# The gate's partition sums of a conditioned short-convolution layer: one fp32 product with ones, or two fp32r products of a high and a low part

## The chip, the core and the metric

The kernel runs on one core of a Trainium2 chip. The core has a matmul engine (PE, whose weight loads are listed apart as PEld), a vector engine (DVE), an activation engine (ACT), GpSimd (POOL), and a queue that issues DMAs (SP). The metric is the device time of one execution in microseconds (us); the median of the runs of a kernel is compared. TensorE is another name for PE.

## What is computed

The reference, cut to the parts that this case runs (one layer, batch 1, 256 rows of 2048):

```python
h = rmsnorm(x, norm_g[0])
mod = silu(c) @ ada_w[0] + ada_b[0]            # 2048 -> 3 * 2048
shift, scale, gate = split(mod, 3)
h = h * (1.0 + scale) + shift
b, cg, v, g = split(h @ sc_w_in[0], 4)         # 2048 -> 4 * 4096
y = b * causal_conv(cg * v, conv_w) * silu(g)  # width 3
x = x + gate * (y @ sc_w_out[0])               # 4096 -> 2048
return rmsnorm(x, final_g)
```

All arrays are float32. The change touches only `gate`: the last third of `silu(c) @ ada_w`, a vector of 2048, which the kernel needs in every partition, since the 256 rows lie in partitions when the gate is applied.

## The kernel before, in words

**Large products.** Each float32 operand is split into a high part, written as fp32r by an ACT cast (`split_hi`, line 318), and a low part, the difference written as fp32r by DVE (`split_lo`, line 323). A product of two operands is then three matmuls: high by high, high by low, low by high (`product`, line 429, and `out_mm`, lines 613 to 615). Weights arrive 1 MB at a time in tiles `raw`, `hi` and `lo` that have three buffers each.

**Stages.** First x is normalized, transposed and modulated with the first shift and scale values. Then comes the first half of the input projection (bank tile `mm_s`), in an order that `plan` works out and that interleaves the shift and scale pieces of `ada_w` (`ada_piece`, line 390 and following). Then comes its second half, a loop over 16 tiles of channels in pairs and the four quarters (`mm_b`, lines 557 to 591), 32 turns in all. The output projection follows in four column blocks dc of 512 (`mm_o`, lines 635 to 690), each over eight pieces of `w_out`.

**The gate.** Each turn of the second half calls `gate_piece` once (line 576). There are 32 pieces: for each of the four column blocks dc, eight pieces of two 128-row blocks of `ada_w`. A piece takes a tile `at_g` from the pool `adap` (tag `at`, four buffers of 1024 floats per partition, shared with the shift and scale pieces, which come before), loads 512 KB into it (line 540, on SP), and adds silu(c) times each of its two rows to the partial sums `gacc` (lines 547 and 549, DVE). `gacc` has tag `gv`, two buffers. After the eighth piece of a block, one matmul of a 128x128 tile of ones with `gacc` adds the 128 partitions up and leaves the sum in every partition (line 552, bank tile `ps_gate`, two buffers shared with other small tiles). DVE adds the bias to it (line 553), and the result, `gate(dc)`, is read at lines 676 (blocks 0 to 2) and 657 (block 3).

**Order.** The instructions of each engine stand in the order that a scheduler gives them when the program is built: it keeps a simulated time, and takes among the instructions that are ready the one with the earliest place in the program. `gate_sums` is called inside `later(GIVE)`, which places its instructions 300 places later than they are written, so that they fill time that is left. On the chip each engine then follows that order.

Of the kernel before, what the change touches and what calls it, by code (L numbers as in the profile page):

```python
# [8 lines left out]
F32 = mybir.dt.float32  # L9
F32R = mybir.dt.float32r  # L10
AF = mybir.ActivationFunctionType
ALU = mybir.AluOpType

P = 128
# [103 lines left out]
def short_conv_layer(ctx: ExitStack, tc: tile.TileContext, x, c, norm_g, ada_w, ada_b, w_in, conv_w, w_out, final_g, out):  # L118
    nc = tc.nc
# [6 lines left out]
    const = ctx.enter_context(tc.tile_pool(name="const", bufs=1))  # L126
    const.tile([P, 48], F32, tag="line0", name="line0")
    adap = ctx.enter_context(tc.tile_pool(name="adap", bufs=2))
# [77 lines left out]
    for n, (j, kk) in enumerate(((0, 4), (4, 4), (8, 4), (12, 2), (14, 1), (15, 1))):  # L206
        at = wpool.tile([P, SLOT], F32, tag=("lo", "hi")[n % 2], name="at0", bufs=3)[:, : kk * 2 * NK0 * P]
        at = at.rearrange("p (k s f) -> p k s f", k=kk, s=2)
# [10 lines left out]

    ident = const.tile([P, P], F32, tag="ident", name="ident")  # L220
    make_identity(nc, ident)
    ones = const.tile([P, P], F32, tag="ones", name="ones")
    nc.vector.memset(ones, 1.0)
    eps_t = const.tile([P, 1], F32, tag="eps", name="eps_t")
    nc.vector.memset(eps_t, EPS)

# [33 lines left out]
    for t in range(TT):  # L260
        for dh in range(2):
# [3 lines left out]
            else:  # L265
                nc.vector.scalar_tensor_tensor(
                    out=junk[:, t], in0=xt[t][dh], scalar=1.0, in1=xt[t][dh], op0=ALU.mult, op1=ALU.mult,
# [58 lines left out]
    def split(raw, n, lo_tag="lo"):  # L326

        return split_lo(raw, n, split_hi(raw, n), lo_tag)
# [4 lines left out]
    gv0 = adap.tile([P, 2, 2 * P], F32, tag="gv", name="gv0")[:, :, 0 : NK0 * P]  # L333
    turn_x(0, 4)

    def sum0(k, rows, col, halves=(0, 1)):


        for o in range(2 * NK0):
            if o // NK0 in halves:  # L340
                nc.tensor.matmul(
                    sums0[:, o * P : (o + 1) * P], rows[:, o // NK0, (o % NK0) * P : (o % NK0 + 1) * P],
                    col.to_broadcast([P, P]),
                    start=k == min(IDLE_AT) and o == 0, stop=k is None, skip_group_check=True,
                )

    for k in range(KT):
        c_k = silu_c[:, k : k + 1]
        at, gv = first_ada[k], gv0
        if k in IDLE_AT:  # L350
# [4 lines left out]
            at, gv = at[:, 1], gv0[:, 1]  # L355
# [2 lines left out]
        else:  # L358
            nc.vector.scalar_tensor_tensor(out=gv, in0=at, scalar=c_k, in1=gv, op0=ALU.mult, op1=ALU.add)
    for half in range(2):  # L360
        sum0(None, gv0, ones[:, 0:1], (half,))
    pieces0 = [split(raw0[:, 0 : CT * P], CT * P)]
    hi0 = [split_hi(raw0[:, k * CT * P : (k + 1) * CT * P], CT * P) for k in range(1, NK0)]
    modulate(0, NK0, sums0.rearrange("p (o f) -> p o f", o=2 * NK0)[:, :, 0])
# [159 lines left out]
    def gate(dc):  # L524
        return gates[dc // 2][:, dc % 2, :]
# [4 lines left out]
    def gate_piece():  # L530
        if not gate_todo:
            return
        dc, j = gate_todo.pop(0)
        at = adap.tile([P, ASLOT], F32, tag="at", name="at_g", bufs=4)
        at3 = at.rearrange("p (k f) -> p k f", k=2)
        with later(GIVE):
            gate_sums(dc, j, at3)

    def gate_sums(dc, j, at3):
        nc.sync.dma_start(at3, adas[:, j : j + 2, 2, dc * 512 : (dc + 1) * 512])  # L540
        if j == 0:
            gacc[0] = adap.tile([P, 512], F32, tag="gv", name="gacc")
        ga = gacc[0]
        for i in range(2):
            s = silu_c[:, j + i : j + i + 1]
            if j + i == 0:
                nc.vector.tensor_scalar_mul(ga, at3[:, i, :], s)
            else:
                nc.vector.scalar_tensor_tensor(out=ga, in0=at3[:, i, :], scalar=s, in1=ga, op0=ALU.mult, op1=ALU.add)
        if j + 2 == KT:  # L550
            ps = psum.tile([P, 512], F32, tag="sm", name="ps_gate", bufs=2)
            nc.tensor.matmul(ps, ones, ga, start=True, stop=True)  # L552
            nc.vector.tensor_tensor(out=gate(dc), in0=ps, in1=gate(dc), op=ALU.add)

    KP = 8
# [79 lines left out]
    for dc in range(4):  # L635
# [10 lines left out]
        for ep in range(n_ep):  # L646
# [7 lines left out]
            if dc == 3:  # L654
# [3 lines left out]
                    out=raw3, in0=raw3, in1=gate(dc).unsqueeze(1).to_broadcast([P, EP, 512]), op=ALU.mult  # L658
# [57 lines left out]
```

## Time and profile before

| | us |
|---|---|
| median of three runs | 925.61 |
| lowest, highest run | 924.23, 926.99 |
| the profiled execution | 925.65 |
| its span, first to last instruction | 923.9 |
| PE busy (98% of the span) | 905.0 |
| DVE busy (67%) | 614.7 |
| ACT busy (50%) | 466.2 |
| the four gate products (line 552), busy as listed | 3.9 |
| gate sums on DVE (lines 547 and 549), 64 instructions | 46.9 |

A group of instructions is one line of the program on one engine with one shape; "x8" is how many there were. A matmul's listed duration runs to a modelled end and overlaps with the next matmul, so what a matmul costs in a stream is read from the distance between starts, or from the chain, the sequence of work traced back from the last instruction. One fp32 matmul in the program shows as two passes in the trace: the four gate products are eight.

### The profile page before, as it was taken

What the parts mean: (1) busy time and instruction counts of PE and PEld (TensorE: products, weight loads), DVE (VectorE), ACT (ScalarE), POOL (GpSimd) and SP (SyncE); (2) the same over time, 40 slices, a digit from 0 to 9 for tenths busy, and PEclk for the clock granted to TensorE, in tenths of its full rate; (3) what the DMA queues carried; (4) which work ended last, traced back from release to release, by engine and by line L of the source; (5) the groups of instructions that cost most, each with busy time, mean ns of one, the idle gap of its engine ahead of it and who ended that gap; (6) DMA issues with size and microseconds to landing.
All of it is one profiled execution on the core that took longest, in us unless ns stands there. A gap on an engine that the chain in (4) does not pass through costs nothing.

```text
span 923.9 us, 16438 instructions
## 1 busy us (share of the span) xinstructions
PE 905.0 (98%) x7135; PEld 870.0 (94%) x7135; DVE 614.7 (67%) x593; ACT 466.2 (50%) x417; POOL 0.7 (0%) x6
## 2 busy tenths in 40 slices
PE   7999999999999999999999999999999999999996
PEld 7898999999999999999999999999999988888885
DVE  4798989897686899875554554455454544545882
ACT  3785876655557856644334333443344333443333
POOL 0000000000000000000000000000000000000000
PEclk9999999999999999999999999999999999999999
DMA  9999999999985789676656665666556496566542
GB/s 314 339 362 326 339 367 366 341 373 357 314 294 180 236 297 355 228 241 205 191 185 197 202 192 185 195 204 194 184 185 199 141 343 225 185 208 200 183 136 92
DMA packets 163753, 227.66 MB, mean 246 GB/s; under 512 B 5680, under 2 KB 104160, under 8 KB 163296
## 3 DMA queue, kind: packets, MB, share of 16 engines
q1 hardware_dynamic: 163440, 226.51, 74.1%
q8 instruction: 56, 0.92, 0.4%
q14 instruction: 17, 0.14, 0.0%
q10 hardware_dynamic: 240, 0.09, 0.0%
HBM read 224.49 MB, written 2.10 MB: 245 GB/s over the span
## 4 chain that ended last, share of the span: by engine, by line
PE 90%; DMA 5%; DVE 2%; issue 1%; SPq 1%; ACT 0%; ACTq 0%; DVEq 0%
PE mm_b L429 38%; PE mm_s L429 33%; PE mm_o L615 6%; PE mm_o L614 6%; PE mm_o L613 6%; DMA at<-in_ada_w_dram 3%; DMA raw_s<-in_sc_w_in_dram 1%; DVE lo L323 1%; DVE gv L412 1%; DMA x<-in_x_dram 1%; PE ps_gate L552 0%; SPq L215 0%; PE tp_g L419 0%; ACT hi L318 0%; DVE gv L410 0%
## 5 line engine op out<-in xcount | busy, mean ns | idle before, releaser
L429 PE MATMUL mm_s<-hT,hi 128*128 128x256 f32 x2048 | 351.7, 277 | 1.6 <-ACT hT L310 1.1
L429 PE MATMUL mm_b<-hT,hi 128*128 128x256 f32 x2048 | 348.8, 276 | 0.0
L429 PEld LDWEIGHTS mm_s<-hT,hi 128*128 128x128 f32 x2048 | 309.6, 189 | 2.5 <-ACT hT L310 1.3
L429 PEld LDWEIGHTS mm_b<-hT,hi 128*128 128x128 f32 x2048 | 308.4, 188 | 0.2 <-issue 0.2
L429 PE MATMUL mm_s<-hT,lo 128*128 128x256 f32 x1024 | 283.6, 278 | 4.0 <-DVE lo L323 3.9
L429 PE MATMUL mm_b<-hT,lo 128*128 128x256 f32 x1024 | 282.6, 276 | 0.0
L323 DVE TENSOR_TENSOR lo<-raw,hi 128x2048 fp32r<-128x2048 f32 (+1 forms) x66 | 148.1, 2244 | 134.6 <-ACT hi L318 134.6
L318 ACT CAST hi<-raw 128x2048 fp32r<-128x2048 f32 (+1 forms) x66 | 123.7, 1874 | 209.0 <-PE mm_b L429 153.3
L429 PEld LDWEIGHTS mm_s<-hT,lo 128*128 128x128 f32 x1024 | 192.5, 188 | 5.2 <-DVE lo L323 4.8
L429 PEld LDWEIGHTS mm_b<-hT,lo 128*128 128x128 f32 x1024 | 192.2, 188 | 0.2 <-issue 0.2
L323 DVE TENSOR_TENSOR lo<-raw_s,hi 128x2048 fp32r<-128x2048 f32 (+1 forms) x80 | 147.9, 1850 | 36.0 <-ACT hi L318 35.2
L318 ACT CAST hi<-raw_s 128x2048 fp32r<-128x2048 f32 (+1 forms) x80 | 124.5, 1557 | 72.3 <-PE mm_s L429 49.1
L323 DVE TENSOR_TENSOR lo<-raw_o,hi 128x2048 fp32r<-128x2048 f32 x32 | 73.3, 2291 | 64.9 <-ACT hi L318 64.9
L318 ACT CAST hi<-raw_o 128x2048 fp32r<-128x2048 f32 x32 | 61.0, 1907 | 106.9 <-PE mm_o L615 83.4
L614 PE MATMUL mm_o<-lo,y 128*128 128x512 f32 x256 | 99.7, 391 | 0.0
L613 PE MATMUL mm_o<-hi,y 128*128 128x512 f32 x256 | 99.3, 389 | 0.0
L615 PE MATMUL mm_o<-hi,y 128*128 128x512 f32 x256 | 99.3, 389 | 0.0
L412 DVE SCALAR_TENSOR_TENSOR gv<-at,silu_c,gv 128x512 f32<-128x512 f32 x105 | 78.5, 750 | 5.5 <-DMA at<-in_ada_w_dram 3.9
L450 ACT COPY acc<-mm_s 128x1024 f32<-128x1024 f32 x54 | 54.6, 1012 | 36.8 <-PE mm_s L429 36.8
L614 PEld LDWEIGHTS mm_o<-lo,y 128*128 128x128 f32 x256 | 48.1, 188 | 10.2 <-issue 0.2
L615 PEld LDWEIGHTS mm_o<-hi,y 128*128 128x128 f32 x256 | 48.0, 188 | 10.0 <-issue 0.2
L613 PEld LDWEIGHTS mm_o<-hi,y 128*128 128x128 f32 x256 | 48.0, 188 | 10.0
(90 smaller groups left out, 368.1 us busy)
## 6 DMA issues: line engine op xcount, KB each, us to landing
raw<-in_sc_w_in_dram SPq DMA_DIRECT2D x64, 1024.0 KB, 5.6
raw_s<-in_sc_w_in_dram SPq DMA_DIRECT2D x47, 1024.0 KB, 8.1
raw_o<-in_sc_w_out_dram SPq DMA_DIRECT2D x32, 1024.0 KB, 5.3
at<-in_ada_w_dram SPq DMA_DIRECT2D x114, 256.0 KB, 7.6
raw_s<-in_sc_w_in_dram SPq DMA_DIRECT2D x33, 512.0 KB, 5.8
at_g<-in_ada_w_dram SPq DMA_DIRECT2D x32, 512.0 KB, 7.9
at<-in_ada_w_dram SPq DMA_DIRECT2D x6, 512.0 KB, 8.8
x<-in_x_dram SPq DMA_DIRECT2D x4, 512.0 KB, 6.0
```

The source lines that it names most:

```text
L318: nc.scalar.copy(hi[:, :n], raw[:, :n])
L323: nc.vector.tensor_tensor(out=lo[:, :n], in0=raw[:, :n], in1=hi[:, :n].bitcast(F32), op=ALU.subtract)
L412: nc.vector.scalar_tensor_tensor(out=gv, in0=at4[:, i], scalar=c_k, in1=gv, op0=ALU.mult, op1=ALU.add)
L429: mm = last_mm[0] = nc.tensor.matmul(dst, w, h[:, k], start=begins and left, stop=ends, skip_group_check=True)
L450: nc.scalar.copy(acc[ch, q], bank)
L613: nc.tensor.matmul(po, yh, hi[:, o], start=opens, stop=False, skip_group_check=True)
L614: nc.tensor.matmul(po, yh, lo[:, o], start=False, stop=False, skip_group_check=True)
L615: nc.tensor.matmul(po, yl, hi[:, o], start=False, stop=ct == NCT - 1, skip_group_check=True)
```

## The change

The tile of ones becomes fp32r. At the end of a block's sums ACT copies `gacc` into the first half of a new tile `parts` as fp32r (the high part), DVE writes the difference into its second half (the low part), and two fp32r products with ones, one of each part, are accumulated in `ps_gate`. The tile `parts` has tag `at`, so it takes one of the four buffers that the pieces of `ada_w` are loaded into. Elsewhere `ones` is read as float32, as before.

```diff
-    ones = const.tile([P, P], F32, tag="ones", name="ones")
-    nc.vector.memset(ones, 1.0)
+    ones = const.tile([P, P], F32R, tag="ones", name="ones")
+    nc.vector.memset(ones.bitcast(F32), 1.0)
...
-        sum0(None, gv0, ones[:, 0:1], (half,))
+        sum0(None, gv0, ones[:, 0:1].bitcast(F32), (half,))
...
             ps = psum.tile([P, 512], F32, tag="sm", name="ps_gate", bufs=2)
-            nc.tensor.matmul(ps, ones, ga, start=True, stop=True)
+            parts = adap.tile([P, 2, 512], F32R, tag="at", name="gate_hl", bufs=4)
+            nc.scalar.copy(parts[:, 0], ga)
+            nc.vector.tensor_tensor(out=parts[:, 1], in0=ga, in1=parts[:, 0].bitcast(F32), op=ALU.subtract)
+            for i in range(2):
+                nc.tensor.matmul(ps, ones, parts[:, i], start=i == 0, stop=i == 1)
             nc.vector.tensor_tensor(out=gate(dc), in0=ps, in1=gate(dc), op=ALU.add)
```

## The prediction

> **What bounds the kernel now.** I read the profile's page first: the busy shares, the granted clock by slices, and the shares of the chain that ended last.
>
> ```profile
> PE 905.0 (98%) x7135; PEld 870.0 (94%) x7135; DVE 614.7 (67%) x593; ACT 466.2 (50%) x417; POOL 0.7 (0%) x6
> ...
> PEclk9999999999999999999999999999999999999999
> ...
> PE 90%; DMA 5%; DVE 2%; issue 1%; SPq 1%; ACT 0%; ACTq 0%; DVEq 0%
> ```
>
> PE is busy for 98% of the span at full granted clock, and 90% of the chain is PE. That is an average, so I read the chain in order of time around the four gate products (columns: start, length, work, matmul passes).
>
> ```profile
> 251.76 62.61 PE mm_s L429 x552
> 314.38 1.72 PE ps_gate L552 x4
> 316.09 76.20 PE mm_s L429 x672
> 392.29 292.17 PE mm_b L429 x2578
> 684.46 0.86 PE ps_gate L552 x2
> 685.32 56.02 PE mm_b L429 x494
> ...
> 763.34 0.86 PE ps_gate L552 x2
> ```
>
> From 251.76 to the last gate product the chain never leaves PE. The four products stand in it in full: two together at 314.38, one at 684.46, one at 763.34. What the change frees on PE there, it frees at the end, unless PE begins to wait. Next, therefore, the waits: those of PE alone between 105 and 740 us, then two of the whole run (total, times, longest).
>
> ```profile
> PE mm_s L429 <- DVE lo L323: 1.2, 1, 1.2
> ...
> DVE lo L323 <- ACT hi L318: 234.8, 112, 7.1
> ACT hi L318 <- PE mm_b L429: 159.8, 48, 4.4
> ```
>
> PE waits once, 1.2 us in 635. The dependence runs the other way: ACT waits 159.8 us for PE to free a high-part buffer, and DVE waits for ACT. The makers of operands stand a full ring of buffers ahead, and that ring is the cover for whatever DVE and ACT get in addition.
>
> **The change part by part.** *Removed:* four fp32 products. Their chain time is 1.72 + 0.86 + 0.86 = 3.44 us, or 0.43 us for each of eight passes.
>
> *Added on PE:* eight fp32r products over 512 columns. The trace has this form in the output projection, where operands are fp32r and each product is one pass of 128x512 (256 of each line). I take the spacing from starts in the timeline:
>
> ```profile
> 759.77 0.39 PE L614 MATMUL mm_o<-lo,y 128*128 128x512 f32 x1
> ...
> 762.49 0.39 PE L614 MATMUL mm_o<-lo,y 128*128 128x512 f32 x1
> 762.72 0.39 PE L615 MATMUL mm_o<-hi,y 128*128 128x512 f32 x1
> 762.95 0.39 PE L613 MATMUL mm_o<-hi,y 128*128 128x512 f32 x1
> 763.17 1.02 PE L552 MATMUL ps_gate<-gacc,ones 128*128 128x512 f32 x2
> 763.63 0.79 PE L614 MATMUL mm_o<-lo,y 128*128 128x512 f32 x1
> ```
>
> The two L614 rows are twelve passes apart (the three lines in turn, four times): 2.72 / 12 = 0.227 us. The listed 0.39 overlaps with the next pass and is no price. Eight passes then take 1.82 us, and PE is relieved by 3.44 - 1.82 = **1.62 us**. The bounds: at the dear end the new pass costs what an old one did, 0.43 us, and nothing is gained; at the cheap end it costs what the 256-column passes of the input projection do, 76.20 / 672 = 0.113 us by the chain, and 8 x 0.113 = 0.91 makes the gain 2.53 us. I take 0.227, since it is the same shape and type.
>
> The Trainium skill (TensorE: Matmul & The Clock Gate, "Back-to-back issue gap") gives a sustained spacing of some 131 ns for 512 columns in a stream of weight loads and matmuls; by that the eight would take an estimated 1.05 us and the gain would be 2.39 us. The trace's 0.227 us in just such a stream disagrees, and the measurement decides.
>
> *Added on ACT and DVE:* four casts and four subtracts of 128x512. Their forms are in the trace as the split of y; the third row is one addition of the gate sums.
>
> ```profile
> L382 ACT CAST y<-z 128x512 fp32r<-128x512 f32 x8 | 4.9, 610 | 0.0
> L383 DVE TENSOR_TENSOR y<-z,y 128x512 fp32r<-128x512 f32 x8 | 5.5, 686 | 0.0
> L549 DVE SCALAR_TENSOR_TENSOR gacc<-at_g,silu_c,gacc 128x512 f32<-128x512 f32 x60 | 45.0, 750 | 1.8 <-DMA at_g<-in_ada_w_dram 1.0
> ```
>
> That is 4 x 0.61 = 2.4 us on ACT and 4 x 0.69 = 2.7 us on DVE. I cost them at nothing: ACT is idle half the span. DVE is tighter in one stretch, so I asked for busy times there (columns: stretch, length, PE, PEld, DVE, ACT, POOL, then clock, DMA share, GB/s).
>
> ```profile
> 277.00:300.00 23.00, 23.00 (x205) 23.00 (x205) 14.27 (x17) 17.03 (x19) 0.00 (x0) 1.00 0.60 182
> ...
> 340.00:392.00 52.00, 52.00 (x461) 52.00 (x460) 48.52 (x54) 34.97 (x34) 0.00 (x0) 1.00 0.89 305
> 392.00:741.00 349.00, 349.00 (x3076) 348.52 (x3075) 186.42 (x141) 142.40 (x107) 0.00 (x0) 1.00 0.61 193
> ```
>
> Even at 93% DVE, between 340 and 392, PE does not wait. If that cover were gone, all of the copy and subtract, 4 x (0.61 + 0.69) = 5.2 us, would be the price.
>
> *New waits.* The subtract waits for the copy at the head of DVE's queue, and the next `lo` and gate additions are queued behind it; the copy can itself stand behind an ACT cast that waits for PE, up to 4.4 us by the wait rows. While ACT waits so, PE still has a ring of finished operands to work through; the wait ends by PE's progress, so it costs nothing. The product waits for the low part, and behind it on PE stand all large matmuls; that is priced among the rivals.
>
> *Moved:* `parts` takes one of the four `at` buffers from the end of a block's sums until its second product is done. The rows of SP's queue and of DVE show what this ring does now:
>
> ```profile
> 271.85 1.94 SPq L540 DMA_DIRECT2D at_g<-in_ada_w_dram  x2
> 277.76 42.06 SPq L472 DMA_DIRECT2D raw_s<-in_sc_w_in_dram  x12
> 321.32 0.37 SPq L540 DMA_DIRECT2D at_g<-in_ada_w_dram  x1
> ...
> 270.29 3.11 DVE L549 SCALAR_TENSOR_TENSOR gacc<-at_g,silu_c,gacc 128x512 f32<-128x512 f32 x4
> ...
> 317.81 0.48 DVE L547 TENSOR_SCALAR gacc<-at_g,silu_c 128x512 f32<-128x512 f32 x1
> ```
>
> The sums of block 1 end at 273.40; block 2 begins only at 317.81, after the products at 314.38 have freed a `gacc`, and loads pause meanwhile. Afterwards the split frees `gacc`, so block 2 may begin before 314; but one or two of the four buffers are then held by `parts` until a product runs, so the gate loads go on with fewer buffers and may spread past 392, where DMA runs at 193 GB/s and DVE is at 53%. Either way they move between stretches in which PE does not wait. On SP a gate load that waits for a buffer holds up the weight loads behind it; their cover is the same ring of three. I cost the move at nothing and keep its failure as a rival.
>
> *The sum.* The profiled execution took 925.65 us (span 923.9 and 1.75 around it), which is the median of 925.61 within 0.04. 925.65 - 1.62 = **924.0 us**, 0.18% less. About 0.3%, or 2.8 us, is what a measurement of this kernel can tell from no change; its three runs lie 2.8 us apart.
>
> **The rivals.**
>
> *A. Nothing saved, 925.6.* PE gains 1.62 us and gives it back in a small wait elsewhere, or the new passes cost 0.43. For it: the order of all engines from 240 us on is made anew. Against it: a single PE wait in 635 us.
>
> *B. Cheaper passes, about 923.1.* The bound of 0.113 us. Against it stand the twelve passes of the same shape at 0.227.
>
> *C. The low part comes late: slower.* PE keeps its order, so if a product is placed soon after its sums, PE stands until cast and subtract are done: worst, behind a full cast and a full low part,
>
> ```profile
> L318 ACT CAST hi<-raw 128x2048 fp32r<-128x2048 f32 x64 | 122.4, 1913 | 201.0 <-PE mm_b L429 153.3 <-issue 43.5 <-PE mm_s L429 4.2
> L323 DVE TENSOR_TENSOR lo<-raw,hi 128x2048 fp32r<-128x2048 f32 x64 | 146.7, 2292 | 134.6 <-ACT hi L318 134.6
> ```
>
> 1.91 + 0.61 + 2.29 + 0.69 = 5.5 us. Once gives 924.0 + 5.5 = 929.5, twice 935. It decides when a product stands less than 5.5 us behind the end of its sums, and makes the kernel slower by over 0.3% from 4.4 us of such waits on. Against it: the products before stood far behind (block 1's sums end at 273.40, its product is in the group at 314.38). For it: blocks 2 and 3 may now be summed late.
> The Trainium skill (TensorE: Matmul & The Clock Gate, the table of specifications) calls ACT's and DVE's queues strictly first in, first out, with only weight loads pulled ahead on PE; by that rule this stall could not be worked around.
>
> *D. Gate loads fall into the opening of the output projection: slower.* There DMA is full and a cast already waits for `w_out`:
>
> ```profile
> 745.00:760.00 15.00, 15.00 (x67) 12.39 (x67) 6.39 (x4) 4.86 (x3) 0.00 (x0) 1.00 1.02 400
> ...
> 756.24 1.91 ACT L318 CAST hi<-raw_o 128x2048 fp32r<-128x2048 f32 x1 [7.46 <-DMA raw_o<-in_sc_w_out_dram]
> ...
> 758.18 2.29 DVE L323 TENSOR_TENSOR lo<-raw_o,hi 128x2048 fp32r<-128x2048 f32 x1 [7.08 <-ACT hi L318]
> ```
>
> That low part is done at 760.47 and first used at 763.63 (the L614 row above): 3.2 us of cover. Eight gate pieces of 512 KB there are 4.2 MB, 10.5 us at 400 GB/s, of which 7.3 reach PE: 931.3; five pieces give 927.4. Against it: block 3 can go on loading once block 2's product is done, near 684.
>
> **How the numbers follow.** Forecast 0.72, A 0.12, B 0.04, C 0.07, D 0.05. The likeliest gives 924.0. The bounds of the pass put the time between 923.1 and 925.65. Before's runs scatter by 1.4 us to either side, a median by less: I reach 0.5 below the lower bound, and 1.35 above the upper, which takes in scatter and a stall short of C's: 922.6 to 927.0. Left out are C, most of D and some scatter. Faster by over 0.3% (under 922.8) needs B and luck, or scatter: 0.05. Slower by over 0.3% (over 928.4) is most of C and D: 0.10. Within 0.3%: 0.85.
>
> **What would show it.** In the profile after: line 552's successors are eight passes, 0.227 us apart where they follow each other, 1.8 us in the chain in place of 3.44; the four casts and subtracts near 0.61 and 0.69 us; PE's waits after 105 us still near 1.2 us in all; gate loads spread differently, and none around 745 to 760. A: passes 0.43 us apart, or a new row "PE ... <- DVE". C: PE waiting for the low part of the gate sums. D: gate loads after 735 and PE waiting for a low part of `w_out`. I am wrong if the chain leaves PE between 252 and 900 us for more than 2 us, or if the stretch before 200 us, which the change does not reach, turns out otherwise.

## The result, and the profile after

The kernel after has a median of **932.29 us** (930.08 to 936.42, six runs) against 925.29 us before (923.42 to 926.99, six runs): a ratio of 1.0079 [1.0053, 1.0104], 7.0 us slower. The profiled execution took 930.08 us, the lowest of its six. From the page of after: busy shares, shares of the chain.

```profile
PE 904.6 (97%) x7135; PEld 870.5 (94%) x7135; DVE 616.8 (66%) x597; ACT 468.5 (50%) x421; POOL 0.7 (0%) x6
PE 87%; DMA 6%; DVE 3%; issue 1%; ACT 1%; SPq 1%; ACTq 0%; DVEq 0%
```

PE is busy for as long as before (904.6 against 905.0 us) in a span of 928.3 us against 923.9, and 3% of the chain has moved from PE to DMA, DVE and ACT. So PE stands somewhere. The chain of after in order of time shows where; before, PE alone filled it from 251.76 to 392.29.

```profile
249.80 0.44 PE tp_g L419 x4
250.24 43.48 PE mm_s L429 x383
...
293.77 0.16 DVE gacc L549
...
294.83 1.22 DVE lo L323
...
301.57 4.81 DMA at_g<-in_ada_w_dram
...
310.96 1.15 DVE lo L323
...
312.12 6.02 DMA raw_s<-in_sc_w_in_dram
...
318.22 1.90 ACT hi L318
320.12 0.93 ACT mm_s L462
...
321.09 76.44 PE mm_s L429 x672
...
397.53 292.40 PE mm_b L429 x2580
689.93 0.23 PE ps_gate L556
...
768.18 0.46 PE ps_gate L556 x2
```

Two things are to be seen. The gate products are cheaper: 0.23 us a pass at 690 (where a second one follows) and at 768. And between 293.72 (250.24 + 43.48) and 321.09 the chain leaves PE, for gate sums, gate loads (`at_g`), a late low part, a late weight load and a late cast. At 321.09 PE still has 672 passes to go to the second half (`mm_b`), as it had before at 316.09, and `mm_b` begins at 397.53 in place of 392.29. The waits of PE and of its weight loads (PEld) between 250 and 330 us (us in all, times, longest; before has none of these rows, and between 330 and 392 neither kernel has one):

```profile
PEld mm_s L429 <- DVE lo L323: 4.5, 3, 2.3
PE mm_s L429 <- DVE lo L323: 3.9, 3, 2.1
...
PEld mm_s L429 <- ACT mm_s L462: 2.8, 1, 2.8
...
PE mm_s L429 <- ACT mm_s L462: 2.5, 1, 2.5
```

DVE's rows there show what a low part stands behind (start, length, work; in brackets the idle time before it and what ended it):

```profile
279.32 0.49 DVE L547 TENSOR_SCALAR gacc<-at_g,silu_c 128x512 f32<-128x512 f32 x1 [2.01 <-DMA at_g<-in_ada_w_dram]
...
292.31 0.75 DVE L549 SCALAR_TENSOR_TENSOR gacc<-at_g,silu_c,gacc 128x512 f32<-128x512 f32 x1 [3.02 <-DMA at_g<-in_ada_w_dram]
...
294.83 1.22 DVE L323 TENSOR_TENSOR lo<-raw_s,hi 128x1024 fp32r<-128x1024 f32 x1
```

Block 2's sums begin at 279.32, not at 317.81: the split has read `gacc`, so its buffer is free early. And they wait for their loads: 3.02 us at 292.31, and the low part of 294.83 stands behind that addition. SP's queue tells why the loads are late:

```profile
271.51 1.40 SPq L540 DMA_DIRECT2D at_g<-in_ada_w_dram  x2
...
280.63 0.37 SPq L540 DMA_DIRECT2D at_g<-in_ada_w_dram  x1
...
283.29 2.99 SPq L540 DMA_DIRECT2D at_g<-in_ada_w_dram  x2
```

A piece's load goes out when an earlier piece has been added: at 280.63, behind the two additions of the first piece; at 283.29, when those of the second end (282.52 + 0.74 in the timeline). The load of 283.29 is the one for which DVE waits until 292.31. Only two of the four `at` buffers turn over. The other two hold the `parts` of blocks 0 and 1, written from 241.7 on, until their products, which stand where they stood:

```profile
L556 PE MATMUL ps_gate<-gate_hl,ones x8: 387/397/398, 314.8 to 768.3; 128*128 128x512 f32 x8
L553 ACT CAST gate_hl<-gacc x4: 609/619/622, 241.7 to 364.2; 128x512 fp32r<-128x512 f32 x4
L554 DVE TENSOR_TENSOR gate_hl<-gacc,gate_hl x4: 684/688/693, 244.0 to 364.9; 128x512 fp32r<-128x512 f32 x4
```

(The columns are shortest, median and longest in ns, then the first and last start.) Adding it up, from the transposes at 250 (`tp_g`; 251.32 before) to the first `mm_b` pass: before 392.29 - 251.32 = 140.97 us; after 397.53 - 249.80 = 147.73. That is +6.76 although the first group of products saves some 0.8 there, so about 7.5 us were lost. PE's rows list 6.4 us of them; since a matmul's listed duration runs past the start of the next, its rows show a gap too short. The weight loads in front of the same four matmuls stood still for 4.5 + 2.8 = 7.3 us, which is nearly the whole loss. The two later groups save 0.79 (0.86 + 0.86 - 0.47 - 0.46), and this execution reached the transposes 1.52 us sooner. That offset is there at 141 us already (139.87 against 141.39), before the first new instruction at 241.7; the twelve profiled executions of this case pass that point anywhere from 137.56 to 143.20. So: 925.65 + 6.76 - 0.79 - 1.52 = 930.10, against 930.08 measured.

### The profile page after: what moved, and what is told of

The parts are those of the page before. It is cut to its first block, busy times and chain, and to the rows that moved or that the text cites. A ratio compares the mean times of both kernels' runs of the same rounds, so it can differ in the third digit from the quotient of the medians.

```text
span 928.3 us, 16457 instructions
## 1 busy us (share of the span) xinstructions
PE 904.6 (97%) x7135; PEld 870.5 (94%) x7135; DVE 616.8 (66%) x597; ACT 468.5 (50%) x421; POOL 0.7 (0%) x6
## 4 chain that ended last, share of the span: by engine, by line
PE 87%; DMA 6%; DVE 3%; issue 1%; ACT 1%; SPq 1%; ACTq 0%; DVEq 0%
PE mm_b L429 38%; PE mm_s L429 30%; PE mm_o L618 6%; PE mm_o L617 6%; PE mm_o L619 6%; DMA raw_s<-in_sc_w_in_dram 3%; DMA at<-in_ada_w_dram 2%; DVE lo L323 1%; DMA x<-in_x_dram 1%; ACT hi L318 1%; DVE gv L412 1%; DMA at_g<-in_ada_w_dram 1%; DVE gacc L549 0%; SPq L215 0%; PE tp_g L419 0%
```

## The experiments

What the traces left open: is it the **early start** of block 2's sums, the **held buffers**, or the **new work itself** (cast, subtract, fp32r products)? And if loads are late, is it their bytes, the buffers, or DVE's additions? Each experiment below is meant to change one of these. Ratios are to the kernel before, on the same chip.

### The sums of a block held back behind the product two blocks before

```diff
-                nc.vector.tensor_scalar_mul(ga, at3[:, i, :], s)
+                first = nc.vector.tensor_scalar_mul(ga, at3[:, i, :], s)
+                if dc >= 2:
+                    tc.add_manual_dep(first.ins, prod[dc - 2].ins.name, held, reason=...)
...
-                nc.tensor.matmul(ps, ones, parts[:, i], start=i == 0, stop=i == 1)
+                prod[dc] = nc.tensor.matmul(ps, ones, parts[:, i], start=i == 0, stop=i == 1)
```

All of the change stays, the held buffers too; only the early start goes.

> The changed kernel, but the first sum of gate block 2 (and 3) also waits for the second product of block 0 (and 1), as it did before the change. Theory 1 (the split frees gacc early, so the additions of block 2 are ordered among the convolution work of the first chunk near 280 to 315 us, stand there at the head of DVE's queue for gate loads that have not landed, and the low parts behind them come late to PE): block 2 starts near 317 again, PE waits for nothing between 200 and 392, and the time is that of the kernel before less the 1.6 us of the passes, 923.7 (925.3 - 1.6). Rival 2 (the tile parts holds two of the four load buffers until the products, so gate loads come late wherever the sums stand): still slower than before, 928 or more, with DVE waiting for gate loads. Rival 3 (the added casts, subtracts and passes cost it themselves): as the changed kernel, 930 to 932.

Measured: 922.44 us against 924.68, ratio 0.9976 [0.9962, 0.9990]. The chain of this kernel is that of before again, with cheaper products:

```profile
251.59 0.44 PE tp_g L419 x4
252.03 62.61 PE mm_s L429 x552
314.64 0.93 PE ps_gate L560 x4
315.58 76.16 PE mm_s L429 x672
391.74 292.40 PE mm_b L429 x2580
684.13 0.24 PE ps_gate L560
...
684.49 0.23 PE ps_gate L560
...
762.38 0.46 PE ps_gate L560 x2
```

The stretch is 140.15 us and PE has no listed wait in it. The products save 0.79 + 0.39 + 0.40 = 1.58 us. So neither the held buffers alone nor the new work costs anything that can be seen. DVE still waits 2.1 us for a gate load at 269.91, in block 1's sums, and PE does not feel it. This is also the version that beats both kernels.

### Early start without the split (I): fp32 products of blocks 0 and 1 placed early

```diff
-            nc.tensor.matmul(ps, ones, ga, start=True, stop=True)
+            with later(-6000 if dc < 2 else 0):
+                nc.tensor.matmul(ps, ones, ga, start=True, stop=True)
```

> The kernel before, with its fp32 products, but the products of blocks 0 and 1 get an early place in PE's order (right behind their sums), which frees gacc early; no split, no tile parts. Theory 1: block 2's additions move to 280 to 315 us and PE waits there, 928 to 933. Rival 2 and rival 3: nothing of what they blame is in it, so as before, 925.3.

Measured: 931.61 us, ratio 1.0063 [1.0044, 1.0082], as slow as after, but by another route. Two of its waits between 250 and 330 us, and its busy times from 277 to 321 us (columns as before):

```profile
PE mm_s L429 <- ACT mm_s L462: 4.3, 1, 4.3
ACT hi L318 <- DMA raw_s<-in_sc_w_in_dram: 3.7, 3, 2.0
```

```profile
277.00:321.00 44.00, 39.69 (x332) 39.50 (x332) 42.43 (x54) 31.82 (x34) 0.00 (x0) 0.93 0.92 312
```

With both `gacc` free early, block 3 comes forward too (its sums begin at 292.01). DVE is full, 42.43 of 44 us; DMA moves 312 GB/s; DVE waits for gate loads for only 2.5 us. So the experiment moved more than it was meant to, and left open which half of it costs. Part of its loss is a lower clock: the 672 passes before the second half take 78.99 us there, against 76.20 before and 76.44 in after.

### Early start without the split (II): only block 0's product placed early

The edit is the same with `dc == 0`. `gacc` is free early for block 2 alone, and no `parts` holds a buffer.

> The kernel before with fp32 products, only block 0's product early: gacc of block 0 is free at 250 us, all four load buffers are free, block 2's additions move to 277 to 321 us, and block 3 stays behind the product of block 1 near 315. If the place of block 2 with four buffers is harmless, and the slowness of the kernel with both products early came from block 3's additions on top (DVE 96% busy there): 924 to 926. If block 2's place alone is enough: 928 to 932.

Measured: 925.65 us against 924.01, ratio 1.0017 [1.0002, 1.0032]; stretch 141.63.

```profile
277.00:321.00 44.00, 43.55 (x378) 42.72 (x378) 40.12 (x48) 33.03 (x36) 0.00 (x0) 1.00 0.87 300
```

Block 2 stands in the same place as in after, DVE is busier there than in after and DMA carries 300 GB/s, and PE has 0.5 us of listed waits. The early start of one block with four buffers costs 0.66 us in the profiled stretch (141.63 - 140.97). The slowness of the experiment before needed block 3 there as well.

### A held buffer without the split

```diff
             ps = psum.tile([P, 512], F32, tag="sm", name="ps_gate", bufs=2)
-            nc.tensor.matmul(ps, ones, ga, start=True, stop=True)
+            parts = adap.tile([P, 2, 512], F32, tag="at", name="gate_hl", bufs=4)
+            nc.scalar.copy(parts[:, 0], ga)
+            nc.tensor.matmul(ps, ones, parts[:, 0], start=True, stop=True)
```

> The kernel before, with ACT copying gacc into a tile parts in a load buffer as float32, and the one fp32 product made from that copy: early release and the held load buffers, without subtract and without fp32r. Theory 1 and rival 2: slow like the changed kernel and 1.6 us more for the fp32 passes, 932 to 934. Rival 3: one copy of 0.6 us in each block, 925 to 926.

Measured: 931.72 us, ratio 1.0072 [1.0047, 1.0097]; stretch 146.92.

```profile
DVE gacc L549 <- DMA at_g<-in_ada_w_dram: 6.9, 5, 2.3
PE mm_s L429 <- DVE lo L323: 3.2, 3, 1.3
```

The same waits as in after (between 250 and 330 us), and 2.3 us more for block 2's first load; here with fp32 products, no subtract and no fp32r operand. What costs is that a copy in an `at` buffer stands in for `gacc`.

### The change with the products of blocks 0 and 1 placed early

The two fp32r products stand inside `later(-6000 if dc < 2 else 0)`. The split still frees `gacc` early, but `parts` is freed early too.

> The changed kernel with the products of blocks 0 and 1 early in PE's order, right behind their low parts, so that parts gives its load buffers back before block 2 begins. If the two held buffers are what makes the loads late: DVE's waits for gate loads near 280 to 320 fall to a few us and the time to 924 to 926. If the additions in that stretch are enough by themselves, as the fp32 kernel with early products suggests: still 928 to 932.

Measured: 924.65 us, ratio 0.9991 [0.9976, 1.0007]; stretch 141.12. Loads on SP, block 2's first sum, and the busy times:

```profile
273.13 5.87 SPq L540 DMA_DIRECT2D at_g<-in_ada_w_dram  x4
```

```profile
280.58 0.49 DVE L547 TENSOR_SCALAR gacc<-at_g,silu_c 128x512 f32<-128x512 f32 x1 [0.58 <-DMA at_g<-in_ada_w_dram]
```

```profile
277.00:321.00 44.00, 43.87 (x384) 43.59 (x384) 40.75 (x51) 31.09 (x33) 0.00 (x0) 1.00 0.88 301
```

The early start is there (280.58), but four loads go out ahead of the sums in place of two, and PE is busy for 43.87 of 44 us. DVE waits 1.8 us for gate loads between 250 and 330 us, against 9.7 in after. A small cost of the early start is left: the stretch is 0.15 us longer than before although its products are some 0.8 cheaper, and the early start with four buffers above cost 0.66. With the first experiment: the loss goes when the early start goes, and it goes when the buffers come back. It needs both.

### Blocks 2 and 3 summed in the second half

The dependence of the first experiment, with the first `mm_b` matmul in place of the product.

> The changed kernel, but the first sums of gate blocks 2 and 3 wait for the first matmul of the second half, so all their additions lie behind 392 us, where DVE is 53% busy. Theory 1: only the place among the convolution work of the chunks costs, so no PE wait between 250 and 740, and 922 to 924, as with the held kernel. If the later place collides with something else (gate loads in the opening of the output projection): above 926.

Measured: 923.87 us against 925.0, ratio 0.9992 [0.9976, 1.0008]; stretch 140.14, no PE wait in it. Moving the sums still later gives nothing beyond the first experiment in the stretch (140.15 there).

### Short loads for block 2

```diff
-        nc.sync.dma_start(at3, adas[:, j : j + 2, 2, dc * 512 : (dc + 1) * 512])
+        w = 64 if dc == 2 else 512
+        nc.sync.dma_start(at3[:, :, 0:w], adas[:, j : j + 2, 2, dc * 512 : dc * 512 + w])
...
+            if dc == 2:
+                row = at3[:, i, 0:64].unsqueeze(1).to_broadcast([P, 8, 64])
```

The order, the additions and the held buffers are those of after; block 2's values are those of 64 columns repeated.

> The changed kernel in the same order of instructions, but the loads of gate block 2 bring only 64 of the 512 columns, and its additions read these eight times over: the additions of DVE stay 128x512 in the same places, and only the loads are shorter; the gate values of that block are not those of the reference. Theory 1, with the wait for loads as the cost: PE's waits between 280 and 325 us go from 6.4 us to under 1.5, 924 to 926. Theory 1 with DVE's additional work in that stretch as the cost: waits stay, 930 to 932. Rival 3: 930 to 932.

Measured: 924.91 us, ratio 1.0001 [0.9989, 1.0013]; stretch 141.10.

```profile
DVE gacc L554 <- DMA at_g<-in_ada_w_dram: 3.4, 2, 2.4
PE mm_s L429 <- ACT mm_s L462: 0.7, 1, 0.7
```

```profile
277.00:321.00 44.00, 43.34 (x378) 42.88 (x377) 41.42 (x50) 34.42 (x39) 0.00 (x0) 1.00 0.69 214
```

The additions in that place do little harm: DVE is busy for 41.42 of 44 us, more than in after, and PE for 43.34. Of DVE's 3.4 us of waits, 2.4 are the one in block 1's sums that the first experiment had too. What costs is the time that block 2's loads take.

### Short loads that are read, long loads that nothing reads

```diff
+        if dc == 2:
+            nc.sync.dma_start(at3[:, :, w:512], adas[:, j : j + 2, 2, dc * 512 + w : (dc + 1) * 512])
```

> The kernel with short loads for gate block 2, in the same order on DVE, but the other 448 columns of each piece are loaded too, by a second DMA behind the short one, and read by nothing; block 2's gate values are not those of the reference. The bytes of the changed kernel are back, the additions still wait for the short loads only. If the price was the additions' wait for their loads at the head of DVE's queue: near the short-loads kernel, 924 to 926, PE waiting under 2 us between 250 and 400. If it was the gate loads' bytes, which delay the weight loads beside them: 930 to 932, with casts waiting for raw_s.

Measured: 930.57 us against 925.0, ratio 1.0048 [1.0028, 1.0067], with runs from 925.26 to 932.13; the profiled one took 931.92, and its stretch is 147.36.

```profile
DVE gacc L556 <- DMA at_g<-in_ada_w_dram: 8.0, 5, 3.4
...
PE mm_s L429 <- DVE lo L323: 3.0, 3, 1.0
```

It was to tell the traffic of the loads from DVE's wait for them, and it does not: with the unread loads beside them the short loads came late as well, and DVE waited as in after. From issue to landing the short loads of block 2 took 1.8 to 8.5 us (median 5.9), against 1.9 to 5.7 (median 3.7) without the unread ones, and SP waited 7.6 us, against 0.5, for earlier loads to land before it could issue the next. The short load for which DVE waits longest (3.44 us, until 293.40) had gone out at 284.83, so it was slow rather than late. That the bytes in flight set the pace is consistent with this, and so is a ring that is too short; the experiment does not separate them.

### The loads without the additions

```diff
-        for i in range(2):
+        for i in range(2 if dc != 2 or j == 0 else 0):
```

> The changed kernel with all its loads, but of gate block 2 only the first piece is added up (14 of the 16 additions of that block are left out, so its gate values are not the reference's); the gate loads stand in SP's order nearly where the changed kernel has them. If the additions waiting in DVE's queue are what delays PE: no PE wait between 250 and 400 us, 922 to 924. If the bytes of the gate loads beside the weight loads are enough: PE waits of some us stay, 928 or more.

Measured: 931.67 us against 924.01, ratio 1.0079 [1.0061, 1.0098]; stretch 151.09. I had expected the loss to go with the additions. It stayed, by a chain of loads:

```profile
284.81 7.12 DMA at_g<-in_ada_w_dram
...
291.94 6.12 DMA at_g<-in_ada_w_dram
```

```profile
ACT hi L318 <- DMA raw_s<-in_sc_w_in_dram: 7.7, 3, 3.5
```

Each load waits at the head of SP's queue for the landing of an earlier one, and the weight loads are behind it on SP: casts wait 7.7 us for `raw_s`, against 0.5 in after. The head of the queue that is blocked has changed from DVE to SP. But this run moved more than the additions: block 2's copy is made at 294.63 already (313.39 in after), so from there three buffers are held until the products at 317.99, and block 3's sums begin at 301.79 (320.15 in after). PE's waits stand from 300 us on, and part of the loss is a lower clock: the 672 passes take 78.08 us, against 76.44 in after. So it shows that the loads can cost as much through SP, not that they do so in after.

### Each fp32 product twice

```diff
-            nc.tensor.matmul(ps, ones, ga, start=True, stop=True)
+            for i in range(2):
+                nc.tensor.matmul(ps, ones, ga, start=i == 0, stop=i == 1)
```

The kernel before, with its sums doubled.

> The kernel before with each fp32 gate product issued twice into the same sum (the gate's sums are doubled). If gate products lie on the path in full, four more cost 3.44 us by the chain: 924.7 + 3.4 = 928.1. If half of that or less is paid, PE's time there is not the end's time, and the 1.6 us of the forecast was mis-sized: 926.5 or less.

Measured: 928.04 us against 925.0, ratio 1.0037 [1.0021, 1.0053], or 3.4 us [1.9, 4.9]; stretch 142.67.

```profile
312.52 3.43 PE ps_gate L553 x8
```

The stretch grows by 1.70 us for four further passes of 0.43, and by nothing else. A gate product is paid in full.

## Why the prediction was wrong

**Right: the price of the products.** The eight new passes cost 0.23 us each; the removed 3.44 us is paid in full (product twice), and the first experiment saves 1.58 of the 1.62 us forecast. Its ratio of 0.9976 is 2.2 us [0.9, 3.5], which holds 1.6.

**Right: the price and the cover of the split.** The cast takes 0.62 us and the subtract 0.69; in the first experiment they stand in the kernel and PE waits for none of them.

**Wrong: the move.** The step that failed is "I cost the move at nothing and keep its failure as a rival." I had seen its parts: that block 2 "may begin before 314", and that "one or two of the four buffers are then held by `parts`". I did not put the two together at one time. From 277 to 315 us block 2's sums run while two buffers are held, and then a load goes out only when an earlier piece has been added. The trace gives the landing times between 270 and 321 us, first before (two loads), then after (eleven; shortest, median, longest):

```profile
DMA to landing us min/median/max: 7.7/7.8/7.9
```

```profile
DMA to landing us min/median/max: 3.6/6.8/8.9
```

The first of these was to be had before the run. A piece needs two additions, 1.5 us by the row of line 549; its load takes 7.8 us. With two buffers a load has for cover only the additions of the other piece and what DVE does between them, and where that is less than the landing time DVE stands. The price of the move was about 7.5 us in the profiled execution, not nothing.

**Wrong: the cover.** I wrote "a gate load that waits for a buffer holds up the weight loads behind it; their cover is the same ring of three", and that PE does not wait "even at 93% DVE". That looked at how busy DVE is, and the run shows it less full than that: 35.34 of 44 us in after, 41.42 with the short loads. What emptied PE's ring was not DVE's work but DVE standing still, with work behind:

```profile
277.00:321.00 44.00, 37.68 (x321) 36.63 (x319) 35.34 (x46) 27.74 (x29) 0.00 (x0) 1.00 0.78 252
```

The waits of DVE for gate loads between 250 and 330 us, behind each of which low parts stand in order, come to 9.7 us. The first of them, 2.4 us at 268.39, is in block 1's sums and costs PE nothing (the first experiment has it too); block 2's four, from 279.32 to 306.47, make 7.3:

```profile
DVE gacc L549 <- DMA at_g<-in_ada_w_dram: 7.7, 4, 3.0
DVE gacc L547 <- DMA at_g<-in_ada_w_dram: 2.0, 1, 2.0
```

The rule of the Trainium skill that rival C cites, DVE's strict first in, first out (TensorE: Matmul & The Clock Gate, the table of specifications), agrees with this trace: no low part passes the addition that waits 3.02 us. The low part of 294.83, whose cast had ended at 290.57, stands behind it. The error lay in applying it only to the new instructions, not to the old ones that the change moves. The last of the stalls then goes round the whole ring: the low part of 310.96 frees a `raw` buffer late, its load goes out at 312.12 and takes 6.02 us, the cast ends at 320.12, the copy into the bank (line 462) is queued behind that cast on ACT, and PE stands 2.5 us for it.

**The rivals.** A did not occur as put: the passes cost 0.23, and the loss is not the saving given back but several times as much. B did not: the passes are not cheaper than 0.227. C did not: no PE wait for the low part of the gate sums is listed, and the products stand some 40 us behind the sums they need (the pair at 314.8 against 274). D did not: the last gate load is issued at 346.8. Slower had 0.10, all of it from C and D; the mechanism that decided was not among the rivals. The sign that I named for being wrong is what the trace shows: "the chain leaves PE between 252 and 900 us for more than 2 us". The stretch before 200 us is the same in kind; its offset of 1.5 us lies within what the opening of these kernels varies by, and no run shows what makes it.

**What stays open.** How much of the 7.5 us is paid in DVE's queue and how much in SP's. In after's trace it is DVE's: `raw_s` loads go out when a low part has freed the buffer, and casts wait 0.5 us for them. But the run without the additions lost as much by way of SP, with a third buffer held, and the unread loads did not separate bytes in flight from buffers. That the early start and the held buffers are needed together is shown; at four buffers the same block in the same place costs 0.66 us.

## What to carry to other kernels

A copy that frees one buffer early and sits in another changes two rings at once: look for the time in which the first lets work start and the second has not yet come back, and count there how many loads can be under way against how long one takes to land. Where an in-order queue waits, price what stands behind the wait, not the busy share of its engine. If a change is good except for the order that it allows, one dependence that restores the old order keeps the gain: here 0.9976 in place of 1.0079.

## What the runs showed that I had not expected

**The granted clock in a stall.** With the two fp32 products early, PE has one listed wait of 4.3 us and the clock from 277 to 321 us is 0.93; in after the longest listed wait is 2.5 us and the clock stays at 1.00. The loads without the additions have 0.96, with PE waits of at most 2.3 us listed:

```profile
277.00:321.00 44.00, 38.16 (x308) 36.83 (x306) 30.15 (x37) 26.51 (x29) 0.00 (x0) 0.96 0.83 275
```

In that last trace two waits stand close together: between 307.06 and 311.00 us PE works on two passes only, and from 311.9 the passes stand about 0.21 us apart in place of 0.113, until about 315.3. From 322.1 to 325.6 they do so again, after a single wait of 2.26 us. The Trainium skill (TensorE: Matmul & The Clock Gate, "What's actually happening") lets the clock fall after an idle window of some 3.4 us; the first two traces agree with it, and the third shows a fall without a wait of that length. These runs don't tell how much work in between still counts as idle.

**The same stretch took more work without loss.** With four buffers, DVE did 40.75 of 44 us of work at 301 GB/s and PE hardly waited; with two, 35.34 us at 252 GB/s cost 7.5 us. Fewer bytes and less work, and slower: what counted for this block was how many loads could be under way. Four buffers do not carry everything: with block 3's sums brought there as well, 42.43 us of work at 312 GB/s, the loss was back by another route.
